# Both squared-relu products by Strassen's seven quarter products, with an accumulating DMA for two weight sums

## The chip, the cores and the metric

The kernel runs on one core of a Trainium2 chip. The metric is device time in microseconds (us). The engines of the core run side by side, each through its own list of instructions in order: TensorE (PE, matmuls), VectorE (DVE), ScalarE (ACT), GpSimd (POOL), and SyncE (SP), which here only issues DMA.

## What is computed

The kernel is a model of two blocks over 16 + 512 tokens of width 1024. The second block has two attentions, each followed by a squared-relu stage:

```
def rms_norm(x, g):
    xf = x.astype(jnp.float32)
    y = xf * lax.rsqrt(jnp.mean(xf * xf, axis=-1, keepdims=True) + EPS)
    return (y * g.astype(jnp.float32)).astype(x.dtype)
...
def sq_relu_mlp(x, w1, w2):
    h = jax.nn.relu(x @ w1)
    return (h * h) @ w2
...
        h = h + sq_relu_mlp(rms_norm(h, mlp_norm[i]), mlp_w1[i], mlp_w2[i])
```

w1 is [1024, 4096] and w2 [4096, 1024], in float32. The first stage (i = 0) takes 528 tokens, the second (i = 1) the last 512.

## The kernel before

The residual h lies in SBUF as [128, 8, 528]: features on the partitions, 8 tiles of them, tokens along the row. A dense product in float32 is made of float32r products: each operand is split into an upper part (a copy in float32r, on ACT) and a lower part (the difference, on DVE), and for each tile of 128 input features PE multiplies upper by upper, upper by lower and lower by upper, which are three matmuls.

A block of 128 outputs takes one load of 512 KB of weights (`wr`, L70, on SP's queue; 3 buffers), the split into `wh` (L82, ACT) and `wl` (L83, DVE; 2 buffers each), and 24 matmuls a bank (L99). In the first stage a block goes through two banks of 264 tokens, in the second (`k.whole`) through one of 512.

`mlp` (L1390 on) is a squared-relu stage. It first calls `before`, the output projection of the attention ahead of it, whose evictions (L857) add to h. Then `operand` splits h times the norm's weights into `xh` and `xl` (L109 on ACT, L110 on DVE, 8 tiles) and adds up the squares of h (L162 on ACT, L163 on POOL). `token_rsqrt` sums them over the partitions by five small matmuls (L171), takes 1 / sqrt by a chain of 12 small DVE operations (L131 to L138, result `rcol`) and turns the result into a row for all partitions by small transposes. The evictions of the first product use that row (L1407: relu times `rs`); then ACT squares (L1410), and L106 and L107 split into `fh` and `fl`. Two chunks of 16 blocks each are followed by `down` (L948), which multiplies a chunk's features with w2, 8 outputs at a time, and adds to h by L857.

The order of the instructions on each engine is set by a scheduler that simulates the program's time when it is built; the code's order is only its input. Each engine then keeps to its list, so an instruction that waits holds up all behind it.

Of the kernel before, what the change touches and what calls it, by code (L numbers as in the profile page):

```python
# [46 lines left out]
class K:  # L47
    """The kernel's context: engines, pools and the pieces that recur."""

    def __init__(self, tc):  # L50
# [4 lines left out]

    def psum(self, **banks):
        """A pool of PSUM banks, so many a tag, for a phase."""
        self.banks = banks
# [27 lines left out]
    def dense(self, wdram, xh, xl, evac, kt=8, lo=0, n=T):  # L86
        """One block of 128 outputs for n tokens, a bank of them at a time: evac(products, tokens) takes them over."""
# [60 lines left out]
    def squares(self, tiles, pool=None, lo=0, eng=None):  # L148
        """Sums over the tiles of their squares from token lo on, [128, tokens] with zeros around."""
# [15 lines left out]
    def sumsq(self, acc, chunks):  # L165
        """The sums over the partitions too, as columns of PSUM (a column a chunk of tokens)."""
# [7 lines left out]
    def rows(self, cols, chunks, take, tags=("pa", "pa")):  # L174
        """The transposes of cols(chunk) [tokens, 128], to take(values, tokens)."""
# [44 lines left out]
# -------------------------------------------------------------------- first layer  # L220
# blocks of w_in: a head's q, k, v, then z, sc_b, sc_c, sc_x, gate_a, gate_b
# [9 lines left out]
class Layer1:  # L231
# [13 lines left out]
    def normed(self, out, lo=0):  # L245
        """Takes over the products of the tokens from lo on with their norm."""
# [47 lines left out]
    def gates(self):  # L294
        """Log decays, their running sums by chunks and betas."""
# [7 lines left out]
        with tc.tile_pool(name="l1g", bufs=1) as pg:  # L303
            G = self.G  # rows 0..15 beta, 32..47 decay; no decay where there is no token
# [118 lines left out]
    def sc_out(self, j):  # L423
        """2 sigmoid(gate_b) y_b for 128 features, in place of the gate."""
# [7 lines left out]
    # ---- independent of the recurrence  # L432
# [7 lines left out]
    def conv_branch(self, j):  # L440
        """sc_b * conv(sc_c * sc_x) for 128 features, in three steps."""
# [47 lines left out]
        # tokens from NM - 4 on, and one of none  # L489
# [7 lines left out]
    def stage_a(self, h):  # L497
        """Projections, convolutions and silu of one head: 2 silu of k and q by chunks, and of v."""
# [37 lines left out]
    def stage_b(self, h, st):  # L536
        """Token-major k and -v, decays, the triangular systems and the inverses of their diagonal blocks."""
# [64 lines left out]
    def levels(self, h, st):  # L602
        """The inverses, block by block, doubled up to the chunk's size."""
# [17 lines left out]
        # blocks of 16: W += W N W between siblings, by way of Q = (W N)^T with a mask  # L621
# [21 lines left out]
        def turn(d, rows, cols):  # L643
            """A block of V as the transpose of W's."""
# [5 lines left out]
        # larger ones start at partitions that a product can take by itself  # L650
        for lv in LEVELS[1:]:
# [3 lines left out]
            def products(d, out, rows, cols, lhs, rhs, eng, pairs=None):  # L655
                """out[rows, cols] = lhs^T rhs for the pairs of blocks."""
# [24 lines left out]
    def stage_c(self, h, st):  # L681
        """The recurrences over the chunks in both directions, the norm and the gate of the output."""
# [1172 lines left out]
```

## Time and profile before

| | us |
|---|---|
| median of 3 runs | 2609.57 |
| lowest, highest | 2607.39, 2611.97 |
| span of the profiled execution | 2607.7 |
| PE busy in it | 2523.1 |
| DVE busy | 1535.0 |
| ACT busy | 1072.2 |
| POOL busy | 438.4 |

The profiled execution has no time of its own beside its span, from the first to the last instruction. It lies 1.9 us under the median of the runs. The mean clock that TensorE was granted is 0.979 of full speed. In the timelines a matmul's duration contains its way through the array, so the time that it costs is the distance between the starts of neighbours.

### The profile page before, as it was taken

How to read it: one execution, taken by the hardware profiler on the slowest of the kernel's cores; microseconds unless marked ns; L12 is line 12 of the kernel's file. 1: busy time of each engine (PE TensorE's matmuls, PEld its weight loads, DVE VectorE, ACT ScalarE, POOL GpSimd, SP SyncE). 2: the span in 40 equal slices, each digit the busy share in tenths (PEclk: the TensorE clock that was granted, in tenths of full speed). 3: DMA queues.
4: the chain of work that ended last, by engine and by line, in shares of the span. 5: the costliest groups of instructions: out<-in, count | busy, mean ns of one | idle time of the engine just before them, and what ended most of it. 6: DMA issues, size and time to landing. Idle time of an engine off the chain costs nothing.

```text
span 2607.7 us, 45619 instructions
## 1 busy us (share of the span) xinstructions
PE 2523.1 (97%) x18012; PEld 2315.5 (89%) x18012; DVE 1535.0 (59%) x3288; ACT 1072.2 (41%) x2191; POOL 438.4 (17%) x599
## 2 busy tenths in 40 slices
PE   8899999999999999999879999999999999999999
PEld 8889999999899888888868999999999988788887
DVE  7878788766554444335998454244555767642432
ACT  5434445353423322333546543133334766431331
POOL 2322212100002111013641010000112444100000
PEclk9999999999999999999978999999999989999999
DMA  4334333524552332333321232223333222232332
GB/s 152 94 95 121 84 96 90 118 89 133 169 204 89 97 97 92 96 90 109 87 71 39 62 114 90 90 89 95 119 95 97 83 72 65 90 95 91 97 105 81
DMA packets 139206, 257.20 MB, mean 99 GB/s; under 512 B 65536, under 2 KB 69664, under 8 KB 138992
## 3 DMA queue, kind: packets, MB, share of 16 engines
q1 hardware_dynamic: 82176, 236.46, 29.2%
q10 hardware_dynamic: 56816, 17.82, 3.5%
q8 instruction: 142, 2.33, 0.4%
q14 instruction: 72, 0.59, 0.1%
HBM read 223.39 MB, written 22.34 MB: 94 GB/s over the span
## 4 chain that ended last, share of the span: by engine, by line
PE 79%; DVE 11%; DMA 3%; ACT 2%; issue 1%; POOL 0%; ACTq 0%; SPq 0%; DVEq 0%; POOLq 0%
PE ps_pd L99 46%; PE ps_pd L948 19%; PE ps_pa L1349 2%; PE ps_po L1664 2%; PE ps_pb L662 1%; DVE prod L839 1%; DVE wl L83 1%; PE ps_pt L1653 1%; PE ps_pt L1339 1%; DVE sc L1280 1%; DVE sc L1268 1%; DMA Dn<-gsc 1%; DVE m L1279 1%; DVE t L1086 1%; DMA blk<-nd 1%
## 5 line engine op out<-in xcount | busy, mean ns | idle before, releaser
L82 ACT ACTIVATE wh<-wr 128x1024 fp32r<-128x1024 f32 (+2 forms) x367 | 379.4, 1034 | 966.7 <-PE ps_pd L99 470.1
L99 PE MATMUL ps_pd<-bigh,wh 128*128 128x256 f32 (+5 forms) x2256 | 695.5, 310 | 17.7 <-ACT bigh L109 6.5
L99 PE MATMUL ps_pd<-bigh,wl 128*128 128x256 f32 (+5 forms) x2256 | 692.5, 308 | 5.4 <-DVE wl L83 5.4
L99 PE MATMUL ps_pd<-bigl,wh 128*128 128x256 f32 (+5 forms) x2256 | 692.5, 308 | 1.2 <-DVE bigl L110 1.0
L83 DVE TENSOR_TENSOR wl<-wr,wh 128x1024 fp32r<-128x1024 f32 (+2 forms) x355 | 429.1, 1209 | 314.9 <-ACT wh L82 308.8
L99 PEld LDWEIGHTS ps_pd<-bigh,wh 128*128 128x128 f32 (+1 forms) x2256 | 430.8, 191 | 39.5 <-ACT bigh L109 6.7
L99 PEld LDWEIGHTS ps_pd<-bigh,wl 128*128 128x128 f32 (+1 forms) x2256 | 430.9, 191 | 24.0 <-DVE wl L83 6.8
L99 PEld LDWEIGHTS ps_pd<-bigl,wh 128*128 128x128 f32 (+1 forms) x2256 | 431.0, 191 | 20.4 <-DVE bigl L110 3.0
L99 PE MATMUL ps_pd<-xh,wh 128*128 128x264 f32 (+1 forms) x1040 | 327.4, 315 | 1.2 <-ACT t L1544 1.2
L99 PE MATMUL ps_pd<-xh,wl 128*128 128x264 f32 (+1 forms) x1040 | 326.4, 314 | 0.8 <-DVE wl L83 0.8
L99 PE MATMUL ps_pd<-xl,wh 128*128 128x264 f32 (+1 forms) x1040 | 325.8, 314 | 0.0
L948 PE MATMUL ps_pd<-fh,wh 128*128 128x264 f32 (+1 forms) x944 | 315.6, 334 | 0.0
L948 PE MATMUL ps_pd<-fh,wl 128*128 128x264 f32 (+1 forms) x944 | 315.6, 334 | 0.0
L948 PE MATMUL ps_pd<-fl,wh 128*128 128x264 f32 (+1 forms) x944 | 315.4, 334 | 0.0
L99 PEld LDWEIGHTS ps_pd<-xh,wh 128*128 128x128 f32 x1040 | 196.7, 189 | 13.8 <-ACT t L1544 2.1
L99 PEld LDWEIGHTS ps_pd<-xh,wl 128*128 128x128 f32 x1040 | 196.8, 189 | 12.7 <-DVE wl L83 1.3
L99 PEld LDWEIGHTS ps_pd<-xl,wh 128*128 128x128 f32 x1040 | 196.9, 189 | 11.7
L948 PEld LDWEIGHTS ps_pd<-fh,wl 128*128 128x128 f32 x944 | 177.2, 188 | 19.5
L948 PEld LDWEIGHTS ps_pd<-fh,wh 128*128 128x128 f32 x944 | 177.2, 188 | 19.5
L948 PEld LDWEIGHTS ps_pd<-fl,wh 128*128 128x128 f32 x944 | 177.3, 188 | 19.3
L163 POOL TENSOR_TENSOR acc<-acc,sq 128x512 f32<-128x512 f32 (+1 forms) x35 | 62.1, 1773 | 602.7 <-ACT sq L162 592.8
L857 DVE TENSOR_TENSOR h<-ps_pd,h 128x256 f32<-128x256 f32 (+3 forms) x112 | 56.2, 502 | 163.9 <-PE ps_pd L948 129.3
(448 smaller groups left out, 3944.2 us busy)
## 6 DMA issues: line engine op xcount, KB each, us to landing
wr<-wm SPq DMA_DIRECT2D x128, 512.0 KB
wr<-w SPq DMA_DIRECT2D x72, 512.0 KB
wr<-wgu SPq DMA_DIRECT2D x44, 512.0 KB
wr<-wa SPq DMA_DIRECT2D x17, 512.0 KB
wr<-wkv SPq DMA_DIRECT2D x17, 512.0 KB
wr<-wdn SPq DMA_DIRECT2D x16, 512.0 KB
wr<-wao SPq DMA_DIRECT2D x16, 512.0 KB
ck<-cd SPq DMA_DIRECT2D x16, 264.0 KB
```

The lines of the kernel that those rows point to most:

```text
L82: nc.scalar.activation(wh, wr, AF.Copy)
L83: (self.low or nc.vector).tensor_tensor(wl, wr, wh, ALU.subtract)
L99: nc.tensor.matmul(ps[:, :half], a[:, k], b[k][:, ts], start=(k == 0 and i == 0), stop=(k == kt - 1 and i == 2))
L163: (eng or nc.vector).tensor_tensor(acc, acc, sq, ALU.add)
L662: nc.tensor.matmul(pq[r, c, :w], lhs(pr)[:, c], rhs(pr)[:, c], start=True, stop=True)
L839: nc.vector.tensor_tensor(prod[:, :i, :i], X[:, :i, :i], bt[:, :i, i].rearrange("p (o j) -> p o j", o=1).broadcast_to([2 * H, i, i]), ALU.mult
L857: k.nc.vector.tensor_add(v, ps, v)
L948: nc.tensor.matmul(pss[h][:, :half], a[:, q], b[f0 + q][:, ts], start=(f0 + q == 0 and i == 0), stop=(f0 + q == nf - 1 and i == 2),)
L1086: nc.vector.tensor_tensor(t, t, sw, ALU.add)
L1268: nc.vector.scalar_tensor_tensor(acc[:n, c0:c1], rl[:n, : c1 - c0], wi[:n, i, hd : hd + 1], acc[:n, c0:c1], ALU.mult, ALU.add)
L1349: nc.tensor.matmul(O[b][:, g], pT[:m, c], self.V[:m, c, 64 * g : 64 * g + 64], start=(c == 0), stop=(c == nch - 1))
L1664: nc.tensor.matmul(po, V[: ns[c], c, par].rearrange("p a n -> p (a n)"), t[: ns[c], c - g], start=(c == 0 and t is hi), stop=(c == nch - 1 ...
```

## The change

The input x of w1 is cut into quarters by halves of the features and halves of the tokens, w1 for a pair of blocks of 128 outputs into quarters by halves of the input features and the two blocks. Instead of eight quarter products seven are made (Strassen's scheme in Winograd's form), of sums of quarters: a pair of blocks takes 7 products of 4 tiles, which is 84 matmuls over half the tokens (264 or 256 columns).

- `combined` makes seven operands for x. Four (b11, b21, b22, t3) lie where xh and xl were; three (t1, t2, t4) in `bigh` and `bigl`, the operand that the output projection ahead still reads. It takes 36 ACT and 44 DVE operations of 264 or 256 columns in place of 8 and 8 of the whole width.
- The weight sums: g2 is loaded with one quarter, twice side by side (L115), and a DMA from POOL's queue adds two other quarters to it (L119, 512 KB), which gives S3 and S1. Two POOL additions of 128x512 make S2 (L120) and S4 (L121). g2 and g4 lie in a pool of their own, `wq`. A pair loads 1.75 MB where two blocks loaded 1 MB.
- A pair's weights are split by 3 ACT and 3 DVE operations of 1024 columns and one each of 512 (L127, L128). Sums of products are taken partly in PSUM, partly by ACT and DVE (`Squares`).
- The factor of the norm moves behind the second product, as its square: two DVE operations (L1557, L1558) in place of L857. So relu and square need no factor.
- Four chunks of 8 blocks in place of two of 16, and the output projection's blocks in the order 0, 4, 1, 5, 2, 6, 3, 7. The weights w1 come from the host as quarters.

The line numbers of the changed kernel are others: L84 there is L83 here, L100 is L99, L169 is L107, L225 is L163, L233 is L171, L193 to L200 are L131 to L138, L919 is L857.

```diff
+    def seven(self, wdram, x, n, evac):
+        nc = self.nc
+        half = n // 2
+        pools = (self.wp, self.wq, self.wp, self.wq)
+        g1, g2, g3, g4 = (p.tile([128, 2, 512], F32, name="wr", tag="wr", bufs=self.wr_bufs - (p is self.wq)) for p in pools)
+        wd = wdram.rearrange("p q k m -> p q (k m)")
+        nc.sync.dma_start(g2, wd[:, 3:4].broadcast_to([128, 2, 512]))
+        nc.sync.dma_start(g4[:, 0], wd[:, 1])
+        nc.sync.dma_start(g1[:, 0], wd[:, 0])
+        nc.sync.dma_start(g3[:, 0], wd[:, 2])
+        nc.gpsimd.dma_start(g2, wd[:, 0:2], accum_op=ALU.add)
+        nc.gpsimd.tensor_tensor(g1[:, 1], g2[:, 0], g4[:, 0], ALU.add)
+        nc.gpsimd.tensor_tensor(g3[:, 1], g1[:, 1], g3[:, 0], ALU.add)
...
+        x1, u, y, v = bank(), bank(), bank(), bank()
+        a11, s2 = part(0, g1, 2)
+        product(x1, a11, "b11")
+        evac.first(x1)
+        product(u, s2, "t2")
+        evac.second(u)
+        s3, s1 = part(1, g2, 2)
+        product(y, s3, "t3")
+        product(v, s1, "t1")
+        evac.third(v)
+        a12, s4 = part(2, g3, 2)
+        product(x1, a12, "b21", start=False)
+        evac.out11(x1)
+        evac.out22(y)
+        z = bank()
+        product(z, s4, "b22")
+        evac.out12(z)
+        (a22,) = part(3, g4, 1)
+        product(y, a22, "t4", start=False)
+        evac.out21(y)
...
 def mlp(k, io, h, i, before, lo=0, n=T):
...
-        xh, xl = ([t[:, :n] for t in tiles(x)] for x in k.operand2())
-        before()
-        acc = operand(k, h, xh, xl, f"mnorm{i}", lo)
...
+        before((0, 4, 1, 5, 2, 6, 3, 7))
...
+        combined(k, h, x, f"mnorm{i}", lo, n, s)
...
+        acc = k.squares(tiles(h), lo=lo, eng=nc.gpsimd)
         rs = token_rsqrt(k, p, acc)
...
+        nc.vector.tensor_tensor(rs, rs, rs, ALU.mult)
...
+                nc.vector.tensor_tensor(y, ps, rs[:, t], ALU.mult)
+                nc.vector.tensor_add(h[:, j, t], h[:, j, t], y)
...
+        for c in range(CHUNKS):
+            f = [[s.tile([128, T], F32R, name=x_, bufs=RING) for x_ in ("fh", "fl")] for _ in range(part)]
+            for j in range(0, part, 2):
+                k.seven(w1[(i * nf + c * part + j) // 2], x, n, Squares(k, s, n, f[j : j + 2]))
+            down(k, w2[8 * i : 8 * i + 8, :, c * part : c * part + part], *zip(*f), part, add, n=n)
...
+CHUNKS = 4
...
-RING = 19
+RING = 10
```

The change also moves instructions. On PE, at the start of the second stage, before (`ps_pd` are the banks of the first blocks, `xh` and `xl` the operand, `acc` the sums of squares):

```order
L99 MATMUL ps_pd_25659<-xh_25373,wl_25656 128x512
L99 MATMUL ps_pd_25623<-xl_25374,wh_25619 128x512
L171 MATMUL ps_pa_25553<-ones1_69,acc_25527 128x1 x5
L99 MATMUL ps_pd_25623<-xh_25373,wl_25620 128x512
L99 MATMUL ps_pd_25659<-xh_25373,wh_25655 128x512
```

And after, where `bigh` and `bigl` are the output projection's operand and `ps_pd_26156` the first of the seven products:

```order
L100 MATMUL ps_pd_25958<-bigl_22014,wh_25954 128x512
L100 MATMUL ps_pd_25958<-bigh_22013,wl_25955 128x512
L233 MATMUL ps_pd_26093<-ones1_69,acc_26067 128x1 x5
L244 MATMUL ps_pd_26115<-idn_66,rcol_26092 128x128 x3
L244 MATMUL ps_pd_26120<-idn_66,rcol_26092 128x128
L244 MATMUL ps_pd_26120<-idn_66,rcol_26092 128x16
L135 MATMUL ps_pd_26156<-xh_25831,wh_26160 128x256
L135 MATMUL ps_pd_26156<-xl_25832,wh_26160 128x256
L135 MATMUL ps_pd_26156<-xh_25831,wl_26161 128x256
```

The sum of squares and the transposes of `rcol` stood among the first blocks' matmuls; now they stand between the output projection's last matmul and the first product.

On DVE, at the same place, before (`h` the eviction of the output projection, `xl` the operand's lower part, `wl` the weights'):

```order
L110 SCALAR_TENSOR_TENSOR xl_25374<-h_9281,params_77,xh_25373 128x512
L83 TENSOR_TENSOR wl_25620<-wr_25617,wh_25619 128x1024
L857 TENSOR_TENSOR h_9281<-ps_pd_25500,h_9281 128x512
L110 SCALAR_TENSOR_TENSOR xl_25374<-h_9281,params_77,xh_25373 128x512
L83 TENSOR_TENSOR wl_25656<-wr_25653,wh_25655 128x1024
L110 SCALAR_TENSOR_TENSOR xl_25374<-h_9281,params_77,xh_25373 128x512
L131 TENSOR_SCALAR rsv_25559<-ps_pa_25553 128x5
L132 TENSOR_SCALAR rst_25560<-rsv_25559 128x5
L83 TENSOR_TENSOR wl_25692<-wr_25689,wh_25691 128x1024
L133 TENSOR_SCALAR rst_25560<-rst_25560 128x5
```

And after, the last rows of `combined` (`gt` and `g22` are its sums) and the first of the rsqrt chain; 26 rows stand between the last eviction into h and `rsv` here, 25 of them of `combined`, in the first stage 24 and 23:

```order
L1505 SCALAR_TENSOR_TENSOR bigl_25970<-gt_26009,bigh_25969 128x256
L169 TENSOR_TENSOR xl_25832<-gt_26053,xh_25831 128x256
L1522 TENSOR_TENSOR g22_26047<-g22_26047,gt_26057 128x256
L169 TENSOR_TENSOR bigl_25970<-gt_26057,bigh_25969 128x256
L1505 SCALAR_TENSOR_TENSOR bigl_25970<-gt_26033,bigh_25969 128x256
L1524 SCALAR_TENSOR_TENSOR gt_26057<-h_9281,params_77,g22_26047 128x256
L1505 SCALAR_TENSOR_TENSOR bigl_25970<-g22_26047,bigh_25969 128x256
L1505 SCALAR_TENSOR_TENSOR bigl_25970<-gt_26057,bigh_25969 128x256
L193 TENSOR_SCALAR rsv_26099<-ps_pd_26093 128x5
L194 TENSOR_SCALAR rst_26100<-rsv_26099 128x5
L195 TENSOR_SCALAR rst_26100<-rst_26100 128x5
L198 SCALAR_TENSOR_TENSOR rsa_26101<-rsv_26099,rst_26100 128x5
```

The chain of rsqrt stood behind the last of eight splits, with weights of the next blocks between; now it stands behind all of `combined`.

On POOL at the same start, after (`wr` are g1 to g4 of the pairs 0 and 1, `acc` the sums of squares of h):

```order
L119 DMA wr_26146<-wm1 128x1024
L225 TENSOR_TENSOR acc_26067<-acc_26067,sq_26071 128x512
L120 TENSOR_TENSOR wr_26145<-wr_26146,wr_26148 128x512
L225 TENSOR_TENSOR acc_26067<-acc_26067,sq_26074 128x512
L119 DMA wr_26281<-wm1 128x1024
L121 TENSOR_TENSOR wr_26147<-wr_26145,wr_26147 128x512
L225 TENSOR_TENSOR acc_26067<-acc_26067,sq_26077 128x512
L120 TENSOR_TENSOR wr_26280<-wr_26281,wr_26283 128x512
L225 TENSOR_TENSOR acc_26067<-acc_26067,sq_26080 128x512
```

Before, only the additions of squares stood there; now the two accumulating DMAs and the four additions of weights stand among them.

## Rows read from the trace of the kernel before

**Rows 1.** The page: span, and an engine's busy time, share, instructions.

```profile
span 2607.7 us, 45619 instructions
...
PE 2523.1 (97%) x18012; PEld 2315.5 (89%) x18012; DVE 1535.0 (59%) x3288; ACT 1072.2 (41%) x2191; POOL 438.4 (17%) x599
```

**Rows 2.** The page, part 4: shares of the chain by engine and line.

```profile
PE ps_pd L99 46%; PE ps_pd L948 19%; PE ps_pa L1349 2%; PE ps_po L1664 2%; PE ps_pb L662 1%; DVE prod L839 1%; DVE wl L83 1%; PE ps_pt L1653 1%; PE ps_pt L1339 1%; DVE sc L1280 1%; DVE sc L1268 1%; DMA Dn<-gsc 1%; DVE m L1279 1%; DVE t L108
```

**Rows 3.** The chain by time (start, us, group), second squared-relu stage.

```profile
2336.82 88.86 PE ps_pd L948 x384
...
2425.67 89.18 PE ps_pd L99 x384
```

**Rows 4.** Windows: busy us and (x count) by engine, PE clock, DMA share, GB/s.

```profile
1525.00:1880.00 355.00, 355.00 (x2920) 354.80 (x2919) 150.37 (x208) 112.63 (x144) 10.22 (x6) 1.00 0.31 96
...
2338.00:2424.00 86.00, 86.00 (x373) 69.71 (x372) 24.83 (x24) 16.75 (x17) 0.00 (x0) 1.00 0.29 94
```

**Rows 5.** Timeline of PE, first squared-relu stage; 15 rows left out between.

```profile
1600.00 0.28 PE L99 MATMUL ps_pd<-xl,wh 128*128 128x264 f32 x1
...
1601.95 0.28 PE L99 MATMUL ps_pd<-xh,wl 128*128 128x264 f32 x1
```

**Rows 6.** Timeline of PE, 256 columns in an earlier stage; 16 left out.

```profile
780.77 0.28 PE L99 MATMUL ps_pd<-mh,wl 128*128 128x256 f32 x1
...
782.81 0.28 PE L99 MATMUL ps_pd<-ml,wh 128*128 128x256 f32 x1
```

**Rows 7.** Timeline of PE, start of the second stage [idle before <-releaser].

```profile
2238.52 0.50 PE L99 MATMUL ps_pd<-bigh,wl 128*128 128x512 f32 x1 [1.49 <-DVE wl L83]
...
2245.91 0.50 PE L99 MATMUL ps_pd<-xh,wl 128*128 128x512 f32 x1 [0.84 <-DVE wl L83]
```

**Rows 8.** Lines by shape, inside the first stage: busy us, mean ns.

```profile
L83 DVE TENSOR_TENSOR wl<-wr,wh 128x1024 fp32r<-128x1024 f32 x57 | 69.9, 1226 | 75.7 <-ACT wh L82 75.7
...
L82 ACT ACTIVATE wh<-wr 128x1024 fp32r<-128x1024 f32 x57 | 60.5, 1061 | 223.4 <-PE ps_pd L99 105.5 <-PE ps_pd L948 102.6 <-issue 15.3
...
L107 DVE TENSOR_TENSOR fl<-u,fh 128x528 fp32r<-128x528 f32 x32 | 22.6, 709 | 1.4 <-ACT fh L106 1.4
...
L106 ACT ACTIVATE fh<-u 128x528 fp32r<-128x528 f32 x31 | 20.1, 647 | 1.0
...
L857 DVE TENSOR_TENSOR h<-ps_pd,h 128x264 f32<-128x264 f32 x26 | 11.2, 433 | 41.7 <-PE ps_pd L948 41.7
```

**Rows 9.** Timeline of DVE, start of the second stage.

```profile
2225.14 0.43 DVE L107 TENSOR_TENSOR bigl<-o,bigh 128x256 fp32r<-128x256 f32 x1 [1.29 <-ACT bigh L106]
...
2235.15 1.77 DVE L110 SCALAR_TENSOR_TENSOR xl<-h,params,xh 128x512 fp32r<-128x512 f32 x1
...
2238.99 0.74 DVE L110 SCALAR_TENSOR_TENSOR xl<-h,params,xh 128x512 fp32r<-128x512 f32 x1
...
2254.90 0.17 DVE L131 TENSOR_SCALAR rsv<-ps_pa 128x5 f32<-128x5 f32 x1 [4.51 <-PE ps_pa L171]
...
2258.25 0.17 DVE L138 SCALAR_TENSOR_TENSOR rcol<-rsa,rcol 128x5 f32<-128x5 f32 x1
```

**Rows 10.** Lines by shape of POOL, start of the second stage.

```profile
L163 POOL TENSOR_TENSOR acc<-acc,sq 128x512 f32<-128x512 f32 x7 | 11.0, 1576 | 14.2 <-ACT sq L162 14.2
```

**Rows 11.** Timeline of SP's DMA queue, the first two weight loads there.

```profile
2238.49 0.33 SPq L70 DMA_DIRECT2D wr<-wm  x1
...
2240.22 0.33 SPq L70 DMA_DIRECT2D wr<-wm  x1
```

**Rows 12.** Timeline of ACT, where these two loads are taken over.

```profile
2242.64 1.05 ACT L82 ACTIVATE wh<-wr 128x1024 fp32r<-128x1024 f32 x1
...
2245.10 1.06 ACT L82 ACTIVATE wh<-wr 128x1024 fp32r<-128x1024 f32 x1 [0.28 <-DMA wr<-wm]
```

**Rows 13.** Windows ahead of the second stage; PE's granted clock follows POOL's count.

```profile
2222.00:2224.00 2.00, 1.08 (x6) 0.66 (x5) 0.71 (x2) 0.54 (x2) 0.07 (x1) 1.00 0.00 0
...
2224.00:2226.00 2.00, 2.00 (x5) 1.56 (x6) 0.43 (x1) 0.42 (x1) 0.66 (x1) 0.53 0.00 0
```

More of the change, by code (lines that the diff above doesn't have):

```diff
@@ L62, in pst @@
     def pst(self, tag="pa"):
+        tag = tag if tag in self.banks else "pd"
         return self.pm.tile([128, 512], F32, name="ps_" + tag, tag=tag, bufs=self.banks[tag])
@@ L100, in products, with part, product, bank @@
             evac(ps[:, :half], slice(h * half, (h + 1) * half))
+    def seven(self, wdram, x, n, evac):
[11 more added lines that the diff above has]
+        nc.gpsimd.tensor_tensor(g3[:, 1], g1[:, 1], g3[:, 0], ALU.add)
+        parts = {}
+        def part(i, g, m):
+            wh, wl = (pools[i].tile([128, 8, 128], F32R, name=x, tag=x, bufs=self.ws_bufs) for x in ("wh", "wl"))
+            v = g[:, :m].rearrange("p q (k m) -> p (q k) m", m=128)
+            nc.scalar.activation(wh[:, : 4 * m], v, AF.Copy)
+            nc.vector.tensor_tensor(wl[:, : 4 * m], v, wh[:, : 4 * m], ALU.subtract)
+            return [(wh[:, 4 * i : 4 * i + 4], wl[:, 4 * i : 4 * i + 4]) for i in range(m)]
+        def product(ps, w, b, start=True):
+            (wh, wl), (bh, bl) = w, x[b]
+            for q in range(4):
+                for i, (a, c) in enumerate(((wh, bh), (wh, bl), (wl, bh))):
+                    nc.tensor.matmul(
+                        ps, a[:, q], c[:, q], start=(start and q == 0 and i == 0), stop=(q == 3 and i == 2),
+                        skip_group_check=not start,
+                    )
+        def bank():
+            return self.pst("pd")[:, :half]
+        x1, u, y, v = bank(), bank(), bank(), bank()
[18 more added lines that the diff above has]
+        evac.out21(y)
@@ L1002, in run, with out @@
             self.attend()
-    def out(self, early=False, js=range(8)):
+    def out(self, js=range(8), early=False):
         k = self.k
@@ L1386, with __init__, first, second @@
 DOUT = tuple(range(40, 56, 2))
+class Squares:
+    def __init__(self, k, s, n, outs):
+        self.k, self.nc, self.s, self.n, self.half, self.outs = k, k.nc, s, n, n // 2, outs
+        self.u = s.tile([128, 2, T], F32, name="u", bufs=2)
+        self.p1, self.u2, self.w = (s.tile([128, T // 2], F32, name=x, bufs=2)[:, : self.half] for x in ("p1", "u2", "w"))
+    def first(self, ps):
+        self.nc.scalar.activation(self.p1, ps, AF.Copy)
+    def second(self, ps):
+        self.nc.vector.tensor_tensor(self.u2, ps, self.p1, ALU.add)
+    def third(self, ps):
+        self.nc.vector.tensor_tensor(self.w, ps, self.u2, ALU.add)
+    def out11(self, ps):
+        self.nc.scalar.activation(self.u[:, 0, : self.half], ps, AF.Relu)
+    def out22(self, ps):
+        self.nc.vector.tensor_tensor(self.u[:, 1, self.half : self.n], ps, self.w, ALU.add)
+    def out12(self, ps):
+        v = self.u[:, 0, self.half : self.n]
+        self.nc.vector.tensor_tensor(v, ps, self.w, ALU.add)
+        self.nc.scalar.activation(v, v, AF.Relu)
+        self.done(0)
+    def out21(self, ps):
+        self.nc.vector.tensor_tensor(self.u[:, 1, : self.half], ps, self.u2, ALU.add)
+        v = self.u[:, 1, : self.n]
+        self.nc.scalar.activation(v, v, AF.Relu, scale=-1.0)
+        self.done(1)
+    def done(self, i):
+        v = self.u[:, i, : self.n]
+        self.nc.scalar.activation(v, v, AF.Square)
+        self.k.split(self.outs[i][0][:, : self.n], self.outs[i][1][:, : self.n], v)
@@ new lines, in combined, with put @@
+def combined(k, h, x, norm, lo, n, pool):
+    nc = k.nc
+    m = n // 2
+    a, b = slice(lo, lo + m), slice(lo + m, lo + n)
+    def put(name, i, v, scale=None):
+        hi, lw = (t[:, i, :m] for t in x[name])
+        if scale is None:
+            k.split(hi, lw, v)
+        else:
+            nc.scalar.activation(hi, v, AF.Copy, scale=scale)
+            nc.vector.scalar_tensor_tensor(lw, v, scale, hi, ALU.mult, ALU.subtract)
+    for i in range(4):
+        p, q = k.par(norm, i), k.par(norm, i + 4)
+        put("b11", i, h[:, i, a], p)
+        put("b21", i, h[:, i + 4, a], q)
+        g22 = pool.tile([128, T // 2], F32, name="g22", tag="fh", bufs=RING)[:, :m]
+        nc.scalar.activation(g22, h[:, i + 4, b], AF.Copy, scale=q)
+        put("b22", i, g22)
+        g12 = pool.tile([128, T // 2], F32, name="g12", tag="fh", bufs=RING)[:, :m]
+        nc.scalar.activation(g12, h[:, i, b], AF.Copy, scale=p)
+        t = pool.tile([128, T // 2], F32, name="gt", tag="fl", bufs=RING)[:, :m]
+        nc.vector.tensor_tensor(t, g22, g12, ALU.subtract)
+        put("t3", i, t)
+        t = pool.tile([128, T // 2], F32, name="gt", tag="fl", bufs=RING)[:, :m]
+        nc.vector.scalar_tensor_tensor(t, h[:, i, a], p, g12, ALU.mult, ALU.subtract)
+        put("t1", i, t)
+        nc.vector.tensor_tensor(g22, g22, t, ALU.add)
+        put("t2", i, g22, -1.0)
+        nc.vector.scalar_tensor_tensor(t, h[:, i + 4, a], q, g22, ALU.mult, ALU.subtract)
+        put("t4", i, t, -1.0)
@@ L1462, in part, with out @@
             k.dense(self.io["wbo"][j][:, a:b], oh[a:b], ol[a:b], residual(k, self.h, NM)(j), kt=b - a, n=S)
-    def out(self):
-        self.part(FPART, 8)
+    def out(self, js):
+        self.part(FPART, 8, js)
     def queries(self):
```

41 lines of the change are left out of this document (26 added, 15 removed).

## The prediction

> **What bounds the kernel now.** I read the page first. TensorE (PE) is busy for 97% of the span [rows 1], and matmuls of L99 and L948, the two products of dense layers, make up two thirds of the chain that ended last [rows 2]. So I then asked of each squared-relu stage whether PE ever waits in it. In the chain the second stage is, from 10 us after its start on, unbroken matmuls of 512 columns, with a piece of 384 for each half of a product; two of them stand in [rows 3]. In a window over the first stage, its start included, PE is busy without a gap, 355.00 of 355.00 us [rows 4]. At the start of the second stage the timeline of PE has two waits, 1.49 and 0.84 us, both for DVE's lower parts of weights [rows 7]. That is all: both stages run at the speed of PE, and every matmul taken away there is time, as long as nothing else becomes late.
>
> **What the change removes.** In the first stage (528 tokens) a pair of blocks took 96 matmuls of 264 columns and now takes 84. The step from one to the next is (1601.95 - 1600.00) / 16 = 0.122 us [rows 5]; 12 x 0.122 x 16 pairs = 23.4 us. In the second stage (512 tokens) a pair took 48 of 512 columns, 89.18 / 384 = 0.232 us each [rows 3], 11.15 us; it now takes 84 of 256, whose step is (782.81 - 780.77) / 17 = 0.120 us [rows 6], 10.08 us. 1.07 x 16 = 17.1 us. Together 40.5 us. The work of the old start goes as well, with its waits of 2.3 us.
>
> **What it adds at the start of a stage.** Before, an operand was 8 splits, and the sum of squares, its rsqrt and the transposes stood between matmuls of the first blocks: DVE did the rsqrt at 2254.90 to 2258.25 [rows 9] while PE went on. Now PE's order has, right behind the last output projection, the sum of squares (L233), the transposes of rcol (L244) and only then the first product (L135); and DVE's order has every row of `combined` ahead of rsv. In the first stage 24 rows of DVE stand between the last update of h and rsv, in the second 26; one of them is a weight's lower part, and twelve write bigl, which the output projection still reads up to its last matmul. PE must wait for all of them. Their price: a 256-column subtraction took 0.43 us [rows 9], and rows that follow each other directly overlap by some 0.07 us, so I take 0.37: 24 x 0.37 = 8.9 us. The weight's lower part: 1.2 [rows 8]. The rsqrt chain, 12 rows from 2254.90 to 2258.25 and 0.17 more [rows 9], took 3.5 us with one weight's subtraction of 1.2 in it, so 2.3 by itself. Sum of squares and transposes: about 1. That is 13.4 us from the last h update. The update itself I let end 1.6 us after its matmul (0.43 of it its own in 264 columns [rows 8], the rest another weight's subtraction that stands just ahead). GpSimd's additions slow DVE: L110 takes 0.74 us alone and 1.77 beside one [rows 9], and seven additions of squares of 1.58 us [rows 10] now have four additions of weights beside them; I take half of what eight L110 lost before, 2.7 us with the weights' subtractions. Last, the accumulating DMA, the two additions of weights and wh stand ahead of wl of pair 0, which stands in DVE's order ahead of the last rows of `combined`: 1.4 us with the DMA's time below. 19.1 us a stage, 38.2 for two; between 13 (rows alone) and 24 (contention full).
>
> PE then starts from idle. At 2222 to 2224 it was busy for 1.08 of 2 us, and the granted clock of the next 2 us was 0.53, near the lower of its two levels, 1.2 GHz [rows 13]. A few microseconds at half speed cost about 2: 4 us for two starts.
>
> The Trainium skill, SBUF — State Buffer, section "SBUF: two separate sides", says that an operation of DVE with two SBUF inputs and one of GpSimd that reads SBUF exclude each other for a whole instruction. The trace agrees: 1.77 against 0.74 us. By that rule taken to the full, eleven additions of 1.58 us would hold DVE up for 17 us a start, and the start would cost about 30.
>
> **The supply of weights.** A pair now loads 1.75 MB instead of 1, and 512 KB of it by an accumulating DMA, which no row of the trace shows. The tag of g2 and g4 has two buffers, so g2 has one: its next load waits until wl of the g2 before is done. The loop is load L, accumulation A, wh 1.06, wl 1.23 [rows 8], and its period must stay within a pair, 10.2 us: L + A up to 7.9. The weights' load issued at 2238.49 was there for wh at 2242.64, 4.15 us later at most; the next, with the first still under way, after 4.88 [rows 11, 12]. I take L = 4.15. For A: nothing says that it is shorter than a plain load, 4.15; and if it reads the destination as well as the source, it takes at most twice the slower load, 9.8. I take 5.5, near the plain load. The loss is 4.15 + 5.5 - 7.95 = 1.7 us a pair, in the pairs 2 and 3 of a chunk (0 and 1 are fetched during the chunk before's second product), 3.4 a chunk, 27 us for eight chunks. Below A = 3.8 it is nothing; at 9.8 it would be 96.
>
> The Trainium skill, DMA: Bandwidth & Descriptors, section "Anatomy of one DMA — SWDGE (gpsimd) path", fits such a DMA with 2.0 us + bytes / 436e3, which for 512 KB is 3.2 us (an estimate by that page). By it the loop would cost nothing. No run here shows an accumulating one.
>
> **What costs nothing, and what covers it.** DVE has 3 subtractions of 1024 columns and one of 512 in a pair (4.3 us), five small evictions (2.2) and two of 0.71 [rows 8], 7.9 of 10.2 us; ACT about as much. Both stay under PE, with little left: 1.5 us of contention is covered, 3 would not be. In the second product two DVE operations take the place of one; DVE is busy for 24.83 of 86 us there [rows 4], so it is covered, apart from the last at the kernel's end, 0.7 us. The squaring of rs is off PE's way. Four chunks instead of two make four more changes between products; now PE passes them without a gap [rows 3], so 0, and 2.6 us each (two of ACT, fh and fl) if the cover is gone, 10 us.
>
> **Sum.** 2607.7 us [rows 1] - 40.5 - 2.3 + 38.2 + 4 + 27 + 0.7 = 2635 us, and the median of the runs is 1.9 us above the profiled span: **2637 us**, 1.0% slower.
>
> **Rivals.**
> *The accumulating DMA is short (faster).* Its place is the loop of g2 and the start of a stage, where DVE's rows wait for it. With A up to 3.8 us the loop costs nothing and the starts lose the 1.4 and part of the waits behind it, 15 each: 2609.6 - 40.5 - 2.3 + 30 + 4 + 0.7 = 2601.5 us. For it: 512 KB came in 4.15 us with an issue and a semaphore in that time. Against: the accumulation must read what it adds to. It decides from A = 4 on; each further us costs 16. Chance 0.20, with starts as low as 13.
> *Between the two (no change).* A of 4 to 4.5 and starts of 16 to 18: 2604 to 2615 us. Chance 0.12.
> *The accumulating DMA takes as long as two loads (much slower).* A of 7 to 9.8 costs 51 to 96 us in the loops and 2 to 4 more at each start: 2665 to 2710 us. For it: twice the traffic at SBUF, and DVE beside it. Chance 0.13.
> *The change doesn't do what it says* (PE's columns take longer in another pattern of banks): 512 and 256 columns stand at 0.232 and 0.120 us, so a column costs the same in both; I give it no chance of its own.
>
> **How the numbers follow.** A forecast between 2615 and 2665 us gets 0.55, and 2637 is its middle. The range 2599 to 2670 leaves out some of the short DMA's case and most of the long one's, less than 2 in 10. The likeliest case alone is 2615 to 2665. About 0.2%, 5.2 us, is what a measurement of this kernel tells from no change: below 2604.4 counts as faster (0.20), above 2614.8 as slower (0.68), between as the same (0.12).
>
> **What would show it.** In the profile after: 84 matmuls a pair at 0.120 to 0.122 us between waits; a gap of PE of 15 to 24 us at each stage's start, ended by DVE's rcol through L244; 24 or so rows of `combined` in that gap; the granted clock near 0.5 behind it; and in pairs 2 and 3 of each chunk a wait of PE of 1 to 2 us for wh or wl that goes back to the accumulating DMA, none in pairs 0 and 1. I am wrong if PE stays busy across the start, if the wait in the loop comes in every pair (then DVE or ACT is the bound), or if it is gone (then the DMA is short).

## The result and the profile after

The changed kernel takes 2716.32 us, median of 4 runs (2709.54 to 2727.85); the kernel before took 2610.77 us beside it. The ratio is 1.0401, with an interval of 1.0367 to 1.0434: slower by 4.0%, where I forecast 1.0%. The profiled execution, 2726.1 us, lies at the upper end of the runs, 11.5 us above the span of their median (2714.6): what is read from its trace runs high by about so much. The seven products are those of the first product of both stages; the second product is made as before, in shorter chunks.

The page of the changed kernel: span, busy times, the chain by engine and by line, the packets of the queue that the accumulating DMAs use (share of 16 engines' span), and the DMA's median from issue to landing.

```profile
span 2726.1 us, 47563 instructions
...
PE 2529.5 (93%) x18396; PEld 2343.1 (86%) x18396; DVE 1731.6 (64%) x3634; ACT 1190.0 (44%) x2439; POOL 570.6 (21%) x695
...
q0 software_dynamic: 4608, 16.78, 3.7%
...
PE 64%; DVE 14%; DMA 10%; issue 5%; ACT 4%; POOL 2%; ACTq 0%; SPq 0%; POOLq 0%; DVEq 0%
...
wr<-wm POOLq DMA_DIRECT2D x32, 512.0 KB, 7.0
```

PE was busy for 97% of the span [rows 1], now for 93%, and 10% of the chain is DMA. The waits of PE over the whole span (in total, times, longest), the lines that the change brought:

```profile
PE ps_pd L135 <- ACT wh L127: 44.5, 16, 5.0
PE ps_pd L233 <- POOL acc L225: 37.3, 2, 18.7
...
PE ps_pd L100 <- ACT wh L83: 10.8, 6, 5.8
...
PE ps_pd L244 <- DVE rcol L200: 4.9, 2, 2.5
```

Sixteen waits in the up phases (the first product) and two at the starts: both places are where I looked for them. A table of where the time went, worked out from the starts of PE's matmuls in each profiled execution (us; an out projection is the one ahead of a stage). The last two columns are experiments that follow below.

| stretch | before | after | two places for g2 | plain first chunk |
|---|---|---|---|---|
| to the end of the first out projection | 1521.7 | 1536.2 | 1538.5 | 1526.4 |
| from there to the end of the first stage | 375.7 | 419.1 | 376.6 | 365.2 |
| to the end of the second out projection | 346.9 | 360.6 | 358.4 | 345.4 |
| from there to the end of the second stage | 359.3 | 405.1 | 371.3 | 352.8 |

After against before: 14.5 and 13.7 us in the stretches that end with an out projection, 43.4 and 45.8 in the stages. Inside a stage, after: 24.8 and 25.2 us between the last output projection and the first product, 199.6 and 197.2 in the up phases (before: 186.7 and 179.2), 194.7 and 182.7 in the second product (before: 187.1 and 177.9).

**The start.** Timeline of PE in the changed kernel, then of POOL and DVE, around the first start:

```profile
1555.05 2.29 PE L233 MATMUL ps_pd<-ones,acc 128*128 128x1 f32 x10 [18.52 <-POOL acc L225]
1559.81 1.33 PE L244 MATMUL ps_pd<-idn,rcol 128*128 128x128 f32 x5 [2.47 <-DVE rcol L200]
```

```profile
1542.01 2.93 POOL L225 TENSOR_TENSOR acc<-acc,sq 128x528 f32<-128x528 f32 x2
1544.90 1.46 POOL L121 TENSOR_TENSOR wr<-wr 128x512 f32<-128x512 f32 x1
...
1551.08 3.92 POOL L225 TENSOR_TENSOR acc<-acc,sq 128x528 f32<-128x528 f32 x1 [1.83 <-ACT sq L224]
```

```profile
1542.26 1.52 DVE L1505 SCALAR_TENSOR_TENSOR bigl<-g,bigh 128x264 fp32r<-128x264 f32 x1
1543.71 1.52 DVE L169 TENSOR_TENSOR bigl<-gt,bigh 128x264 fp32r<-128x264 f32 x1
...
1552.74 0.42 DVE L169 TENSOR_TENSOR xl<-gt,xh 128x264 fp32r<-128x264 f32 x1
...
1555.78 0.43 DVE L1505 SCALAR_TENSOR_TENSOR bigl<-gt,bigh 128x264 fp32r<-128x264 f32 x1 [0.49 <-ACT bigh L1504]
1557.38 0.16 DVE L193 TENSOR_SCALAR rsv<-ps_pd 128x5 f32<-128x5 f32 x1 [1.17 <-PE ps_pd L233]
```

PE stands for 18.52 us at L233, as the order of the instructions had it, then again for rcol. POOL's last addition of squares ends at 1555.00, DVE's last row of `combined` at 1556.21: two paths of nearly one length, of which the prediction let PE wait for DVE's alone. A row of 0.42 us on DVE takes 1.52 while POOL adds: what [rows 9] showed for larger rows. Eight such rows in the first gap and seven in the second took 8.7 and 7.4 us more than at 0.43. POOL's last addition takes 3.92 us in place of 1.5, while the rows of DVE beside it run at 0.42 up to 1553.77. The out projection is late too. Ahead of the second start, ACT first and then PE:

```profile
2301.35 1.58 ACT L127 ACTIVATE wh<-wr 128x1024 fp32r<-128x1024 f32 x2 [5.48 <-DMA wr<-wm]
2302.83 0.51 ACT L83 ACTIVATE wh<-wr 128x384 fp32r<-128x384 f32 x1
```

```profile
2303.39 0.80 PE L100 MATMUL ps_pd<-bigh,wh 128*128 128x512 f32 x1 [5.83 <-ACT wh L83]
```

The upper part of g2 (L127) stands in ACT's order ahead of the out projection's next weights (L83). It waits 5.48 us for the accumulating DMA, and PE waits with it.

**The loop of g2.** The last chunk of the first stage; SP's queue (L115 loads g2), POOL (L119 adds to it) and ACT:

```profile
1867.32 0.38 SPq L115 DMA_DIRECT2D wr<-wm  x1
...
1880.61 0.38 SPq L115 DMA_DIRECT2D wr<-wm  x1
```

```profile
1872.02 0.88 POOL L119 DMA_DIRECT2D wr<-wm  x1 [11.80 <-DVE fl L169]
...
1885.35 0.88 POOL L119 DMA_DIRECT2D wr<-wm  x1 [3.67 <-DVE wl L128]
```

```profile
1878.18 1.06 ACT L127 ACTIVATE wh<-wr 128x1024 fp32r<-128x1024 f32 x1 [5.05 <-PE ps_pd L135]
...
1893.59 1.06 ACT L127 ACTIVATE wh<-wr 128x1024 fp32r<-128x1024 f32 x1 [6.27 <-DMA wr<-wm]
```

From one load of g2 to the next are 13.29 us: 4.70 to the accumulation's issue, 6.1 to its landing, the rest the two parts. The next accumulation takes 8.2. What SP's queue (q1) brought in the meantime, with packets, MB and share, first from 1872.02 to 1878.09, then from 1885.35 to 1893.51:

```profile
q1 hardware_dynamic: 206, 0.36, 20.4%
```

```profile
q1 hardware_dynamic: 286, 0.77, 39.0%
```

Over all 32 accumulations, those beside at most 0.53 MB landed after 5.5 to 7.2 us, those beside 0.56 to 0.78 MB after 7.2 to 8.2, those beside 1.2 to 1.4 MB after 7.5 to 9.2. A pair of PE lasts 10.2. In the matmuls' rows, pairs 0 and 1 of every chunk wait for nothing, pair 2 waits 1.2 to 2.7 us, pair 3 2.7 to 5.0. Behind such a wait PE runs slowly; windows of the first chunk (PE busy; PE's granted clock is the third figure from the end):

```profile
1594.00:1596.00 2.00, 0.83 (x7) 0.62 (x6) 0.00 (x0) 0.10 (x1) 0.10 (x1) 1.00 0.53 104
1596.00:1598.00 2.00, 0.00 (x0) 0.00 (x0) 1.01 (x1) 2.00 (x3) 1.92 (x2) 0.88 0.02 4
1598.00:1600.00 2.00, 1.70 (x7) 1.71 (x8) 2.00 (x3) 0.83 (x2) 1.38 (x1) 0.50 0.23 75
1600.00:1602.00 2.00, 2.00 (x11) 2.00 (x11) 1.96 (x4) 1.97 (x5) 0.00 (x0) 0.50 0.89 199
```

PE was idle for some 3 us and was then granted 0.50, the lower level of 1.2 GHz, up to about 1604. The granted clock fell to 0.50 behind the wait of pair 3 in each of the eight chunks, behind that of pair 2 in two. In the up phases of a stage the steps between matmuls are 12.9 and 12.7 us longer than at full clock, apart from the waits; 3.0 us of that lie in the first pairs behind the two starts, which leaves 2.8 us a chunk.

### The profile page after: what moved, and what is told of

It is laid out like the page before. It is cut to its first block, busy times and chain, and to the rows that moved or that the text cites. A ratio compares the mean times of both kernels' runs of the same rounds, so it can differ in the third digit from the quotient of the medians.

```text
span 2726.1 us, 47563 instructions
## 1 busy us (share of the span) xinstructions
PE 2529.5 (93%) x18396; PEld 2343.1 (86%) x18396; DVE 1731.6 (64%) x3634; ACT 1190.0 (44%) x2439; POOL 570.6 (21%) x695
## 4 chain that ended last, share of the span: by engine, by line
PE 64%; DVE 14%; DMA 10%; issue 5%; ACT 4%; POOL 2%; ACTq 0%; SPq 0%; POOLq 0%; DVEq 0%
PE ps_pd L100 29%; PE ps_pd L1010 17%; DMA wr<-wm 6%; PE ps_pd L135 4%; PE ps_pa L1411 2%; PE ps_po L1821 1%; DVE wl L84 1%; ACT wh L127 1%; DVE wl L128 1%; DVE prod L901 1%; PE ps_pb L724 1%; DMA Dn<-gsc 1%; DMA wd<-Xt 1%; PE ps_pt L1401 1%; DVE sc L1342 1%
## 5 line engine op out<-in xcount | busy, mean ns | idle before, releaser
L100 PE MATMUL ps_pd<-bigh,wh 128*128 128x256 f32 (+5 forms) x2256 | 696.8, 310 | 24.8 <-ACT wh L83 10.8
L100 PE MATMUL ps_pd<-bigh,wl 128*128 128x256 f32 (+5 forms) x2256 | 693.6, 309 | 4.7 <-DVE wl L84 4.7
L100 PE MATMUL ps_pd<-bigl,wh 128*128 128x256 f32 (+5 forms) x2256 | 693.4, 308 | 1.7 <-DVE bigl L172 1.5
L83 ACT ACTIVATE wh<-wr 128x1024 fp32r<-128x1024 f32 (+3 forms) x303 | 311.3, 1028 | 662.4 <-PE ps_pd L100 270.7
L100 PEld LDWEIGHTS ps_pd<-bigh,wh 128*128 128x128 f32 (+1 forms) x2256 | 431.5, 192 | 48.3 <-ACT wh L83 12.2
L100 PEld LDWEIGHTS ps_pd<-bigh,wl 128*128 128x128 f32 (+1 forms) x2256 | 431.5, 192 | 24.0 <-DVE wl L84 6.7
L84 DVE TENSOR_TENSOR wl<-wr,wh 128x1024 fp32r<-128x1024 f32 (+3 forms) x291 | 352.2, 1211 | 154.4 <-ACT wh L83 147.1
L100 PEld LDWEIGHTS ps_pd<-bigl,wh 128*128 128x128 f32 (+1 forms) x2256 | 431.3, 191 | 21.5 <-DVE bigl L172 3.9
L128 DVE TENSOR_TENSOR wl<-wr,wh 128x1024 fp32r<-128x1024 f32 (+1 forms) x128 | 152.9, 1197 | 119.9 <-ACT wh L127 118.2
L127 ACT ACTIVATE wh<-wr 128x1024 fp32r<-128x1024 f32 (+1 forms) x128 | 120.9, 949 | 234.0 <-DMA wr<-wm 118.3
L135 PE MATMUL ps_pd<-xh,wh 128*128 128x264 f32 (+1 forms) x512 | 152.9, 302 | 44.5 <-ACT wh L127 44.5
L135 PE MATMUL ps_pd<-xh,wl 128*128 128x264 f32 (+1 forms) x512 | 150.4, 297 | 1.2 <-DVE wl L128 1.0
L135 PE MATMUL ps_pd<-xl,wh 128*128 128x264 f32 (+1 forms) x512 | 151.3, 296 | 0.0
L135 PEld LDWEIGHTS ps_pd<-xh,wh 128*128 128x128 f32 x512 | 103.6, 203 | 48.0 <-ACT wh L127 47.8
L1557 DVE TENSOR_TENSOR y<-ps_pd,rrow 128x264 f32<-128x264 f32 (+1 forms) x96 | 49.4, 518 | 143.2 <-PE ps_pd L1010 143.2
L225 POOL TENSOR_TENSOR acc<-acc,sq 128x512 f32<-128x512 f32 (+1 forms) x35 | 63.8, 1821 | 257.3 <-ACT sq L224 257.1
```

Source lines behind the costliest of these rows:

```text
L83: nc.scalar.activation(wh, wr, AF.Copy)
L84: (self.low or nc.vector).tensor_tensor(wl, wr, wh, ALU.subtract)
L100: nc.tensor.matmul(ps[:, :half], a[:, k], b[k][:, ts], start=(k == 0 and i == 0), stop=(k == kt - 1 and i == 2))
L127: nc.scalar.activation(wh[:, : 4 * m], v, AF.Copy)
L128: nc.vector.tensor_tensor(wl[:, : 4 * m], v, wh[:, : 4 * m], ALU.subtract)
L135: nc.tensor.matmul(ps, a[:, q], c[:, q], start=(start and q == 0 and i == 0), stop=(q == 3 and i == 2), skip_group_check=not start,)
```

## The experiments

All are edits of the changed kernel. Theory: the loop of g2 with its long accumulation, and the order at the start, are two separate stalls. Rivals: the accumulation isn't the matter, but DVE, ACT and POOL are too slow for a pair; DVE's rows hold the start whatever the order. The kernel before took 2606.8 us beside runs 1 to 4, 2612.3 beside 5 to 8, 2609.1 beside 9 to 11 and 2610.3 beside 12, so a difference of some 6 us between runs of different groups says nothing, and the runs of the changed kernel themselves lie up to 18 us apart.

**1. Without the accumulating DMA.**

```diff
-        nc.gpsimd.dma_start(g2, wd[:, 0:2], accum_op=ALU.add)
```

> Leaves out the accumulating DMA (so two of the weight sums are not formed; the plain loads and every matmul stay). Theory (the loop of g2: load 4.7 us, accumulation 6 to 8, parts 2.4, one place in the buffer): PE's waits for wh in the up phases fall from 44 us to under 8, the slow-clock loss behind them from 25 to under 8, the out projection before the second start stops waiting for wh behind it; about 2640 us. Rival (DVE, ACT and GpSimd together hold up a pair): the waits stay above 30 us, about 2700 us.

Measured 2640.5 us. Of the waits for wh in the up phases 3.1 us were left, of the slow clock 2.6. The gaps at the starts stayed, 22.7 and 24.5 us. So the accumulating DMA costs some 76 us in all, and with two additions a pair on POOL, DVE, ACT and POOL keep up with PE.

**2. The same DMA without adding.**

```diff
-        nc.gpsimd.dma_start(g2, wd[:, 0:2], accum_op=ALU.add)
+        nc.gpsimd.dma_start(g2, wd[:, 0:2])
```

> The same DMA from the same queue at the same place, but it overwrites instead of adding (two weight sums are not formed). If the adding is what is dear: issue to landing falls from 7.0 us to about 4, waits in the up phases under 15 us, about 2655 us. If the software queue is what is dear: landing stays at 6 us or more and the time at 2700 us or above.

Measured 2671.9 us, between the two. Its queue and its landing, on the page:

```profile
q0 software_dynamic: 4608, 16.78, 1.9%
...
wr<-wm POOLq DMA_DIRECT2D x32, 512.0 KB, 5.0
```

For the same bytes the engines were busy for 1.9% in place of 3.7% of the span, and it landed in 5.0 us in place of 7.0. The waits in the up phases fell to 20 us. Adding costs 44 us, a plain DMA at this place still 31: it stands in the loop behind the load, whatever it does.

**3. Two places for g2.**

```diff
-        g1, g2, g3, g4 = (p.tile([128, 2, 512], F32, name="wr", tag="wr", bufs=...) for p in pools)
+        g1, g3 = (self.wp.tile([128, 2, 512], F32, name="wr", tag="wr", bufs=self.wr_bufs) for _ in range(2))
+        g2 = self.wq.tile([128, 2, 512], F32, name="wg", tag="wg", bufs=2)
+        g4 = self.wq.tile([128, 1, 512], F32, name="wf", tag="wf", bufs=2)
-RING = 10
+RING = 9
```

> g2 gets two places instead of one (g4 two of half the size, ring of features 9 instead of 10), all else as changed. Theory: the load and the accumulation of the next pair run during the pair before, so the waits in the up phases go under 10 us although the accumulation still takes 7 us; 2645 to 2660 us. Rival (the accumulation or GpSimd's queue is short of throughput): the waits stay above 30 us, 2700 us or more.

Measured 2650.6 us. The accumulation still landed after 6.9 us (median), but PE waited in no pair, and the up phases took 164.2 and 161.1 us: 16 pairs at 10.24 and 10.08 would be 163.8 and 161.3. So it was the one place that made the accumulation's time count, for 66 us of the 105. What is left of PE's waits stands at the starts:

```profile
PE ps_pd L235 <- POOL acc L227: 36.4, 2, 19.1
PE ps_pd L100 <- ACT wh L83: 14.1, 6, 7.0
```

**4. The norm later.** The squares, sum, rsqrt and transposes are written behind pair 1 of the first chunk; the factor is needed only behind the second product.

```diff
-        acc = k.squares(tiles(h), lo=lo, eng=nc.gpsimd)
-        rs = token_rsqrt(k, p, acc)
-        nc.vector.tensor_tensor(rs, rs, rs, ALU.mult)
...
                 k.seven(...)
+                if c == 0 and j == 2:
+                    acc = k.squares(tiles(h), lo=lo, eng=nc.gpsimd)
+                    rs = token_rsqrt(k, p, acc)
+                    nc.vector.tensor_tensor(rs, rs, rs, ALU.mult)
```

> The squares, the sum, rsqrt and transposes are written behind the second pair of the first chunk, all else as changed. Theory (PE's order puts the sum of squares ahead of the first product, and the sum waits for GpSimd): of the 24.6 us between the last output projection and the first product at each start under 10 remain, 2675 to 2690 us. Rival (the rows of the combined operands on DVE hold the first product anyway): 15 us or more remain, 2700 us or more.

Measured 2698.0 us. The gap is gone, 0.13 and 0.23 us in place of 25. But the first pair takes 21.6 and 23.0 us in place of 11.2 and 11.6, with waits for xl and bigl, and rcol holds PE for 9.7 us in all. Of some 50 us only 18 are won: by its time the rival was near, since DVE's rows hold PE as soon as the order doesn't. Both are true, one behind the other.

**5 and 6. Two places and the later norm**, behind pair 1 (`j == 2`) and behind pair 2 (`j == 4`).

> Two places for g2 and the norm's squares behind the second pair of the first chunk. If the two stalls are independent: 2650 us (two places alone) less the 18 us that the late norm alone brought, about 2632 us, and no wait for wh in pairs 2 and 3. Rival (behind the late norm the loop had hidden more, since DVE's backlog only moves into the first chunk): 2640 us or more.

> As the run before, the squares behind the third pair. If the additions of squares on GpSimd hold DVE up while it still has rows of the combined operands: fewer waits in the first chunk, 2620 to 2628 us. If the first chunk is held up by the 44 rows themselves: the same as behind the second pair, within 4 us.

Measured 2632.5 and 2634.6 us. Within the noise the gains of 3 and 4 add up, so the stalls are separate; and where the squares stand in the first chunk makes no difference. The first pair takes 21.5 to 24.2 us in both, with waits for the operands and for weights that stand behind them in DVE's order. That the 44 rows of `combined` fill it I take from these waits; run 12 moves them.

**7. Two places, squares added on DVE.**

```diff
-        acc = k.squares(tiles(h), lo=lo, eng=nc.gpsimd)
+        acc = k.squares(tiles(h), lo=lo)
```

> Two places for g2; the additions of squares on DVE instead of GpSimd, the norm still ahead of the first product. If DVE and GpSimd exclude each other (rows of 0.41 us that take 1.48 us at the start): the gap from the last output projection to the first product falls from 24 us to about 17 (ten such rows give back 10 us, seven additions of 0.7 us cost 5, and the last addition of GpSimd, 3.8 us, goes), 2635 to 2642 us. If the rows alone make the gap: it grows, 2650 to 2660 us.

Measured 2641.0 us, 9.6 less than with two places alone, within what I expected, but not where: the gaps are 22.9 and 25.4 us (25.5 and 25.6 there), and 5.4 and 2.4 us were won ahead of the gaps, in the out projections. Of the rows of `combined` in the gaps two and one still took 1.5 us, beside POOL's additions of weights, where in run 3 seven and six had taken that or more; the others took 0.41 to 0.48. So that the two exclude each other is shown; what it gave back in the gap the added squares mostly took, three of which took 1.8 us beside POOL.

**8 and 10. Both sums on POOL, no accumulating DMA**, with the norm later (8) and with the norm ahead as in the change (10). A pair loads 1 MB; g4's free half takes the quarter that g2 was loaded with.

```diff
-        nc.sync.dma_start(g2, wd[:, 3:4].broadcast_to([128, 2, 512]))
         nc.sync.dma_start(g4[:, 0], wd[:, 1])
+        nc.sync.dma_start(g4[:, 1], wd[:, 3])
...
-        nc.gpsimd.dma_start(g2, wd[:, 0:2], accum_op=ALU.add)
+        nc.gpsimd.tensor_tensor(g2[:, 0], g1[:, 0], g4[:, 1], ALU.add)
+        nc.gpsimd.tensor_tensor(g2[:, 1], g4[:, 0], g4[:, 1], ALU.add)
```

> No accumulating DMA: both sums are two more additions of 128x512 on GpSimd from plain loads of 1 MB a pair, g2 with one place again; norm behind the second pair. If the loop of the DMA is all that the up phases wait for: no waits in pairs 2 and 3, 2620 to 2635 us. If four additions a pair, which exclude DVE, fill DVE's time: waits in every pair, 2660 us or more.

> The sums on GpSimd, the norm ahead of the first product as in the change: what the accumulating DMA alone costs, with nothing left out. Theory: the up phases wait for nothing, the starts stay at 24 us or a little more (three or four more additions on GpSimd beside DVE): 2640 to 2652 us.

Measured 2627.6 and 2637.4 us, the second a little under what I expected. Run 10 leaves nothing out and takes 79 us less than the changed kernel: the clearest price of the accumulating DMA. No pair of chunks 1 to 3 waits, although POOL now makes four additions a pair. With the norm ahead the gaps are 29.0 and 27.2 us, the longest of all: what run 10 loses, it loses at the starts and, by 5.4 and 3.4 us, in the out projections ahead of them.

**9 and 11. The products in another order**, on 8: those with operands in xh and xl (b11, t3, b21, b22) first, then t2, t1, t4; the squares behind pair 1 (9) and pair 2 (11).

> As the run with the sums on GpSimd and the norm behind the second pair, and of the seven products of a pair the four whose operands lie in xh and xl (b11, t3, b21, b22) come first, the three that wait for the output projection's operand (t2, t1, t4) last. If the first pair waits for the twelve rows that write bigl: pair 0 of each first chunk, now 23 to 25 us, takes 14 to 18, and the whole 2612 to 2620 us. If weights and DVE's whole backlog hold it: no change within 5 us of 2627 us.

> As the run with the reordered products, the squares behind the third pair instead of the second, when DVE's backlog is gone: 0 to 8 us faster than that run if GpSimd's additions of squares still collide with DVE in the first chunk, else the same.

Measured 2675.3 and 2669.1 us, 48 and 41 us slower than 8, which I had not expected; the 6 us between the two lie within the spread of each. The first pair stays at 25.6 and 23.2 us, but that doesn't show whether bigl holds it: the scheduler changed the order there. The code has 48 matmuls ahead of the first from bigh, PE's list in run 9 only 23 and 20, where run 8 has 12 and 2. PE in run 9, where the first of them starts:

```profile
1537.02 0.42 PE L136 MATMUL ps_pd<-xh,wl 128*128 128x264 f32 x1
1537.24 0.64 PE L136 MATMUL ps_pd<-bigh,wh 128*128 128x264 f32 x2
```

The question stays open. And now every chunk waits. The waits of PE from 1660 to 1890 us, in chunks 1 to 3 of the first stage, in run 9:

```profile
PE ps_pd L136 <- DVE u L1473: 6.0, 3, 2.0
PE ps_pd L136 <- DVE wl L129: 2.0, 3, 0.9
```

L1473 is the eviction of y. In this order y and z are begun early and evicted last, so that a pair has up to four banks of PSUM open almost to its end, and of eight banks the next pair, which opens five, gets four at most. That the banks are the reason I take from that wait; no run gave it more banks.

**12. The first chunk plain.** Eight products of quarters (96 matmuls a pair) in chunk 0, with a quarter b12 in the place of t3; t1 to t4, the squares and rsqrt are made during that chunk; chunks 1 to 3 as in 8.

```diff
+                if c:
                     k.seven(w1[(i * nf + c * part + j) // 2], x, n, Squares(k, s, n, f[j : j + 2]))
+                else:
+                    k.four(w1[(i * nf + j) // 2], x, n, s.tile([128, 2, T], F32, name="u", bufs=2), f[j : j + 2])
+                    combined(k, h, xx, f"mnorm{i}", lo, n, s, (j // 2,))
```

> The first chunk of each stage by eight plain products of quarters (96 matmuls a pair), from a fourth quarter b12 that takes the place of t3; the four combined operands t1 to t4, the squares and rsqrt are made during that chunk; chunks 1 to 3 by seven products with the sums on GpSimd and no accumulating DMA. Ring of features 9. If the starts cost what they do because the combined operands and the norm stand ahead of the first product: PE has work across the start as before the change, three quarters of the 40 us gained stay, less a few us: 2580 to 2592 us, faster than before. If DVE's 32 rows in the first chunk hold PE up all the same: 2600 to 2620 us.

Measured 2596.6 us, a ratio to before of 0.9954 (0.9937 to 0.9970): faster than both kernels, less than I expected. The waits of PE in its first stage:

```profile
PE ps_pd L283 <- DVE rcol L239: 4.3, 1, 4.3
PE ps_pd L185 <- DVE xl L1544: 0.7, 1, 0.7
```

The gap at the start is gone and the out projections are nearly as before (table above). What keeps it from 2580 to 2592 is among others the wait for rcol, behind which the clock falls once more, and the second products of the second stage, 5.2 us longer than before.

## Why the prediction was wrong

The direction, the two places (the loop of g2 and the starts) and their mechanisms were right. The term of the loop was far too small, that of the starts somewhat, and the out projections had no term; so the time lies beyond the range. From the forecast's span, 2635 us, to the profiled one are 91 us. The loop costs 71.5 in the up phases where I had 27, the out projections 28.2 where I had none, the second products 12.4 where I had 0.7, the starts 50.0 where I had 38.2. Less the 4 us for the slow clock behind the starts, which the up phases contain, these differences come to 92.

**The gain on PE** was right. In run 3, where nothing waits, the up phases are 22.5 and 18.1 us shorter than before, 40.6 in all; the prediction had 40.5. That they are equal to 0.1 us is luck: the 40.6 still contain some 3 us of slow clock in the first pairs, for which the prediction had 4 apart.

**The supply of weights** is the step that failed most: "I take 5.5, near the plain load" for A, and 4.15 for L. Measured in the pairs that count, A is 6.1 to 7.2 us in pair 2 and 7.2 to 8.2 in pair 3, L 4.7. The formula itself holds: with means of 6.6 and 7.4 it gives 3.3 and 4.2 us, 60 us for eight chunks, where I had 27. By the medians two places save 66 us, by the profiles, from which these landings are, 71.5 in the up phases. The remainder I put down to the clock; no run separates it. I priced a start from idle, but not that a wait of 3 to 5 us in the loop brings the clock down in the same way. The rows from which I chose A were plain loads with at most one other under way; the accumulation moves as many bytes with nearly twice the engine time (3.7% against 1.9%), and lands the later the more the other loads bring beside it. The Trainium skill (DMA: Bandwidth & Descriptors, section "Anatomy of one DMA — SWDGE (gpsimd) path") fits a DMA on this path with 2.0 us + bytes / 436e3, which I weighed as an estimate of 3.2 us for 512 KB. The trace doesn't agree: the plain DMA of run 2 took 4.0 to 7.4 us among the other loads, the accumulating one 5.5 to 9.2; the measurement decides, and the rule alone would have put me further off.

**The starts.** The order (L233 and L244 ahead of the first product) was read rightly, and run 4 shows that it makes the gap. The term was 19.1 us a start and is 24.8 and 25.2, over the upper bound of 24 too. Part of it is the tail: sum, rsqrt and transposes, which I had at 3.3 us, take 6.0 from 1555.05 to the first product, in part because the granted clock is 0.50 there. Part is the exclusion of DVE and POOL: I took 2.7 us, half of what the old start showed, and it took 8.7 and 7.4; the other terms came out a little smaller. The Trainium skill (SBUF — State Buffer, section "SBUF: two separate sides") says that the exclusion holds for a whole instruction. The rows of 1.52 us agree with it, but its full price of 17 us a start was some twice what they cost.

**What no term held** are the out projections, 14.5 and 13.7 us. I counted what stands behind the last update of h, and not what `combined` and the first weights put ahead of the out projection's own weights on ACT and DVE. Run 1 leaves 6.3 and 9.3 us of the delay, run 10 leaves 5.4 and 3.4: half of it or more goes with the accumulating DMA, for which ACT waits there. With two places (run 3) 16.8 and 11.5 us stay. What the rest consists of no run separates.

**What I took as covered** was not all covered. In the changed kernel the second products are 7.6 and 4.8 us longer than before, 3.9 and 3.7 of it waits. With two places the first stage's excess is gone, so it came from the loop. That of the second stage stays: in run 3 the second products are 6.6 us longer in all, with waits of 4.8 for wh and wl of w2, where I had 0 with a bound of 10 for all changes between products. The clock is not in it: it was 1.00 from 2302 us of run 3 on (third figure from the end).

```profile
2302.00:2644.00 342.00, 337.27 (x2095) 299.90 (x2095) 206.32 (x266) 152.93 (x220) 48.89 (x40) 1.00 0.46 126
```

**The rivals.** The long accumulating DMA, with 0.13, is nearest: I gave it 2665 to 2710 us for A of 7 to 9.8. But A was 7.0 in the mean of pairs 2 and 3, its lower end, for which I had 2665; that the time comes out near its upper end, 6 us above, is not its doing but that of the out projections, the starts, the second products and the clock. The short one is excluded by its landings of 5.5 us and more.

With the measured terms, from the profile of before to that of run 3: 2607.7 - 40.6 (matmuls) + 51.1 (gaps) - 3.6 (the sums and transposes that stood among the blocks) + 28.3 (out projections) + 6.6 (second products) = 2649.5 us, and the span is 2649.9. This is bookkeeping: the terms are differences of the same two traces. The changed kernel's span is another 76.2 us longer, of which 71.5 lie in its up phases.

## What to carry to other kernels

Count the places that a buffer has before costing a transfer as hidden: a chain of load, accumulate and split costs its full excess over the compute with one place (13.3 us against a pair's 10.2), and cost nothing here with two. Where PE is the bound, a wait can cost its length and then the slower clock behind it: the sixteen waits of the loop, 44.5 us, came with 22.6 us of slower steps. A faster algorithm that needs more preparation should begin with the old one: give PE a plain piece of work while the combined operands and the norm are made.

## What the runs showed of the hardware

The accumulating DMA of 512 KB took nearly twice the engine time of a plain one from the same queue (3.7% against 1.9% of the span for 32 of them), and landed 2 us later in the median; it landed after 5.5 to 7.2 us beside at most 0.53 MB of other loads, after 7.5 to 9.2 beside 1.2 to 1.4 MB. A DVE subtraction of 264 columns with both inputs in SBUF took 0.42 us alone and 1.52 beside a POOL addition. After a wait of 3.5 us, from 1594.8 to 1598.3, PE's granted clock was 0.50 up to about 1604.
